# A decoder layer on one core: normed latents stored in full, and split where they are loaded

## The chip, the cores and the metric

The kernel runs on one core of a Trainium2 chip. A core has TensorE for matrix products (PE in the profile, its weight loads PEld), VectorE (DVE), ScalarE (ACT), GpSimd (POOL), and SyncE (SP), which here only issues DMAs; each works through its own queue of instructions in order and waits for the others by semaphores. The metric is the device time of one execution in microseconds (us); before the change it was 1661.43 us in the median of three runs.

## The reference

One layer of a decoder trunk on 1024 tokens of width 1024, all in float32: a norm with a conditioned scale and shift, two mixers side by side, a gated merge, a feed-forward part, a final norm. The part at hand is the second mixer, a latent attention:

```python
proj = h @ w_in
a_qkv, c_q, c_kv, k_r, gate_a, gate_b = jnp.split(proj, IN_SPLIT_POINTS, axis=-1)
y_a = _dilated_attention(a_qkv, rel_bias) @ w_up_a
y_b = _mla(c_q, c_kv, k_r, positions, g_q_lora, w_uq, g_kv_lora, w_ukv) @ w_up_b
...
# _mla
q = jnp.einsum('bsl,lhd->bshd', _rmsnorm(c_q, g_q_lora), w_uq)
kv = jnp.einsum('bsl,lhd->bshd', _rmsnorm(c_kv, g_kv_lora), w_ukv)
q_nope, q_rope = q[..., :M_NOPE], _rope(q[..., M_NOPE:], positions)
k_nope, v = kv[..., :M_NOPE], kv[..., M_NOPE:]
k_rope = _rope(k_r, positions)
```

The query latent `c_q` has 768 columns, the key/value latent `c_kv` 256: six and two pieces of 128. Both mixers have eight heads of width 64.

## The kernel before

A float32 operand is split into a high part, rounded to the format of the fast matrix product, and a low part, the rest; a product is three matmuls (high by high, high by low, low by high). `split` does this with a cast on ACT (line 83) and a subtraction on DVE, or on POOL where it is told so (line 84). A tile of 128 by 1024 float32 is 512 KB, half a tile (`hf`, 512 tokens) 256 KB.

Stage 1 is the input projection, in nine groups of two column pairs. Each pair is a Strassen product of seven (line 171: order 0, 1, 5, 4, 6, 3, 2), each with 12 matmuls at line 220. Products 5, 6 and 3 of a pair add up in one PSUM bank, and between them ACT or DVE copies out what has been reached (`plus`, `keep`). The right-hand operands lie in numbered cells of SBUF: product 4 reads cells 0 to 3, product 6 cells 4 to 7, product 3 cells 8 to 11, product 2 cells 12 to 15, product 5 cells 16 to 19. Sigmoid gates go to DRAM (`god`, line 399), and so do the latents. `cq_out` multiplies a piece of the query latent by its gain, splits it, and stores both parts in `nqd[0]` to `nqd[5]`. `kv_norm` does it for the two pieces of the key/value latent (`nqd[6]`, `nqd[7]`), normed in full.

Stage 2 is the attention: 16 heads (0 to 7 dilated, 8 to 15 latent), four units of 256 queries each, so units 0 to 63. A unit computes scores (`S`), exponentials on ACT (`P`), transposes (`tr`) and the product with the values (`pv`). A generator of fill work, `fill_a`, is drawn on during units 0 to 31 and puts other matmuls between (`acc`): `f_uk1` makes the keys of the latent heads in eight half tiles, `f_vb` their values in eight blocks of 128 tokens, stored to `vbd`, and `f_uq` their queries. Its operands are the latents, which `load_n` fetches into cells by way of POOL's DMA queue (`ldr`). `others` issues the loads of the next head at the second unit of each head, and at unit 1 the six query pieces and `k_rope`, which rotates the shared key. The key weight `wuk` is loaded by SP and split by ACT and POOL (`wk`).

The order of each engine's queue is not written by hand. A scheduler sorts the instructions by a timing model of its own and gives them their places; `tc.issue_after(x)` adds an edge from `x` to those instructions of the block that are on `x`'s engine.

Of the kernel before, what the change touches and what calls it, by code (L numbers as in the profile page):

```python
# [19 lines left out]
F32 = mybir.dt.float32  # L20
# [3 lines left out]
OP = mybir.AluOpType  # L24
# [20 lines left out]
def layer_kernel(ctx: ExitStack, tc: tile.TileContext, xT, c, pos, relT, wada, bada, gains, gq, gkv,  # L45
# [36 lines left out]
    def split(src, hi, lo, eng=DVE):  # L82
        ACT.copy(hi, src)  # L83
        eng.tensor_sub(lo, src, f32(hi))  # L84
# [52 lines left out]
    cqd = [dp.tile([P, T], F32, name=f"cqd{j}") for j in range(2)]  # L137
    nqd = [dp.tile([2, P, T], F32, name=f"nqd{j}") for j in range(8)]
    god = [dp.tile([P, T], F32, name=f"god{g}") for g in range(16)]
# [201 lines left out]
    def cq_out(src, j, hf, inplace):  # L341
        if hf not in acc:
            acc[hf] = SG()
            ACT.activation(acc[hf], src, AF.Square)
        else:
            t = X()
            ACT.activation(t, src, AF.Square)
            DVE.tensor_add(acc[hf], acc[hf], t)
        hi = X(F32R)
        lo = src.bitcast(F32R) if inplace else X(F32R)  # L350
        ACT.activation(hi, src, AF.Copy, scale=gql[:, j:j + 1])
        DVE.scalar_tensor_tensor(lo, src, gql[:, j:j + 1], f32(hi), op0=OP.mult, op1=OP.subtract)
        st(nqd[j][0][:, hsl[hf]], f32(hi))
        st(nqd[j][1][:, hsl[hf]], f32(lo))

# [291 lines left out]
    def kv_norm(hf, ts):  # L647
        a, b = SG(), f32(CHI())
        ACT.activation(a, ts[0], AF.Square)
        ACT.activation(b, ts[1], AF.Square)  # L650
        DVE.tensor_add(a, a, b)
        ps = trb()
        rms_rows(rms_cols([a], 256, ps), ps)
        for i, t in enumerate(ts):
            hi = CHI()
            DVE.scalar_tensor_tensor(t, t, gql[:, 6 + i:7 + i], ps, op0=OP.mult, op1=OP.mult)
            split(t, hi, t.bitcast(F32R))
            st(nqd[6 + i][0][:, hsl[hf]], f32(hi))
            st(nqd[6 + i][1][:, hsl[hf]], t)

# [59 lines left out]
    with ExitStack() as s2:  # L720
# [146 lines left out]
        wcols = lambda w: [t.rearrange("p (k f) -> p k f", f=P) for t in w]  # L867
        NHOME = (0, 2, 4, 6, 8, 10, 16, 18)
        nt = {}

        def load_n(j):
            t = [cell(NHOME[j] + l, [P, T]) for l in range(2)]
            for l in range(2):
                ldr(t[l], nqd[j][l])
            nt[j] = t

# [34 lines left out]

        OHOME = (12, 14, 16, 18)
        oa = {}
# [37 lines left out]
        def fill_a():  # L951
            small = [f_uk1(j, hf) for j in range(4) for hf in range(2)] + [f_vb(tb) for tb in range(8)]
            big = [f_uq(j, hf) for j in (4, 0, 1, 5, 2, 3) for hf in range(2)]
            pat = cycle("ssq")
            while small or big:
                kind = next(pat)
                src = small if kind == "s" and small or not big else big
                yield from src.pop(0)

# [7 lines left out]
        for j in (6, 7):  # L967
            load_n(j)
        cur["uk"] = wcols(wsplit(wuk, T, wraw(wuk, T, cell(4, [P, T], F32))))
        osum = {}  # L970
# [3 lines left out]
        def open_unit(u):  # L974
# [6 lines left out]
            units[u] = Unit(heads[idx], I, osum[0], 64 * (idx % 2), idx)  # L981

        def others(u):
            idx, I = u // 4, u % 4
            if I == 1 and idx < 15:
                heads[idx + 1] = load_head(*seq[idx + 1], (idx + 1) % 2)
            if u == 1:
                with tc.issue_after(v_ins[0].ins):
                    for j in (0, 1, 3, 4, 5, 2):
                        load_n(j)  # L990
                k_rope()

# [450 lines left out]
```

## Time and profile before

| | us |
|---|---|
| three runs | 1661.43, 1657.0, 1661.94 |
| the profiled execution | 1654.69 |
| its span | 1652.9 |
| PE busy | 1530.0 (93%) |
| DVE busy | 1237.9 (75%) |
| ACT busy | 828.9 (50%) |
| POOL busy | 549.9 (33%) |

Times inside the span count from its start. A row of the timeline gives the start, the duration, the engine, the line, the operation, output and inputs, and in brackets how long the engine stood idle before and what ended that. A row of the windows gives the length of a stretch and the busy time of each engine with its count of instructions, then the clock granted to PE (1.00 is full), the share of the DMA engines that was busy, and GB/s. A row of waits gives who waited for whom, the total in us, how many times, and the longest. Stage 1 ends near 434.5 us, and the dilated heads run from there to 657.6 us.

### The profile page before, as it was taken

Reading aid. Unit: us, or ns where it says so; the run is one execution under the profiler, and the core shown is the slowest. Engines: PE = TensorE matmul, PEld = TensorE weight load, DVE = VectorE, ACT = ScalarE, POOL = GpSimd, SP = SyncE. Lnnn points to the kernel's source line nnn. Section 1 sums busy time; section 2 is a strip of 40 time slices with the busy share of each in tenths; the row PEclk is TensorE's granted clock in tenths of the full one; section 3 lists DMA queues with packets and bytes.
Section 4 is the critical chain, followed back from the end, with each engine's and each line's share of the span. In section 5 each row is a group of like instructions: output and inputs, shape, how many; then the busy total and the mean of one; then the engine's idle time right before and its main releaser. Section 6 shows DMA issues by size and latency. Waiting matters only on the chain.

```text
span 1652.9 us, 22277 instructions
## 1 busy us (share of the span) xinstructions
PE 1530.0 (93%) x7306; PEld 1273.5 (77%) x7306; DVE 1237.9 (75%) x2443; ACT 828.9 (50%) x1631; POOL 549.9 (33%) x505
## 2 busy tenths in 40 slices
PE   4988999999769998999999997999999999899996
PEld 2757778878657887999978886778888888688885
DVE  7987997576267767889867669687767677688887
ACT  5842425444366867777734454434444444222325
POOL 0142333224243546434132015432332333233323
PEclk8989999999889999999999998999999999999998
DMA  9539675458996977766285342444444447966412
GB/s 336 187 120 328 241 254 198 146 185 240 284 228 171 220 200 203 181 164 153 69 307 202 133 141 73 169 185 179 159 148 160 166 145 283 393 251 256 176 41 102
DMA packets 175364, 321.40 MB, mean 194 GB/s; under 512 B 36988, under 2 KB 72492, under 8 KB 170000
## 3 DMA queue, kind: packets, MB, share of 16 engines
q1 hardware_dynamic: 107088, 241.22, 42.7%
q0 software_dynamic: 48000, 42.04, 12.0%
q10 hardware_dynamic: 20160, 36.71, 5.9%
q8 instruction: 58, 0.95, 0.2%
q14 instruction: 58, 0.48, 0.1%
HBM read 222.20 MB, written 102.34 MB: 196 GB/s over the span
## 4 chain that ended last, share of the span: by engine, by line
PE 49%; DVE 6%; DMA 6%; ACT 2%; issue 2%; POOL 1%; ACTq 0%; DVEq 0%; POOLq 0%; SPq 0%
PE bk L220 29%; PE acc L892 3%; PE S L783 3%; PE bk L87 3%; PE bk L89 3%; PE bk L88 3%; PE pv L824 2%; PE tr L805 2%; DMA vbd<-ev 2%; DMA tod<-x 1%; DMA cell<-tod 1%; DVE Wop L84 1%; DVE cell L84 1%; DMA Wraw<-wgate 1%; DVE x L278 1%
## 5 line engine op out<-in xcount | busy, mean ns | idle before, releaser
L220 PE MATMUL bk<-cell,Wop 128*128 128x512 f32 x4056 | 946.3, 395 | 44.7 <-DVE x L233 13.0
L220 PEld LDWEIGHTS bk<-cell,Wop 128*128 128x128 f32 x4056 | 769.3, 190 | 215.8 <-DVE Wop L84 11.5
L190 POOL TENSOR_TENSOR Wsum<-Wraw 128x512 f32<-128x512 f32 (+1 forms) x120 | 158.6, 1324 | 597.0 <-DVE Wop L84 377.3
L83 ACT CAST Wop<-Wsum 128x512 fp32r<-128x512 f32 (+1 forms) x241 | 130.0, 548 | 220.1 <-PE bk L220 159.4
L83 ACT CAST Wop<-Wraw 128x512 fp32r<-128x512 f32 (+2 forms) x182 | 107.6, 593 | 173.5 <-PE bk L220 99.5
L84 DVE TENSOR_TENSOR Wop<-Wsum,Wop 128x512 fp32r<-128x512 f32 (+1 forms) x241 | 157.8, 663 | 46.7 <-ACT Wop L83 46.1
L84 DVE TENSOR_TENSOR Wop<-Wraw,Wop 128x512 fp32r<-128x512 f32 (+2 forms) x182 | 138.6, 765 | 34.5 <-ACT Wop L83 32.2
L783 PE MATMUL S<-cell,cell 128*128 128x128 f32 (+8 forms) x480 | 120.0, 365 | 13.1 <-DMA cell<-ksd 8.3
L1245 DVE SCALAR_TENSOR_TENSOR x<-bk,modc,x 128x512 f32<-128x512 f32 x140 | 103.5, 747 | 35.8 <-PE bk L220 30.9
L790 ACT ACTIVATE P<-P,mx 128x512 f32<-128x512 f32 (+7 forms) x128 | 99.4, 779 | 34.9 <-DVE mx L785 21.6
L84 DVE TENSOR_TENSOR pl<-tr,ph 128x512 fp32r<-128x512 f32 (+1 forms) x160 | 98.4, 630 | 24.3 <-ACT ph L83 23.4
L892 PE MATMUL acc<-cell,w 128*128 128x512 f32 x408 | 112.7, 404 | 0.1
L190 POOL TENSOR_TENSOR Wsum<-Wraw,Wsum 128x512 f32<-128x512 f32 (+1 forms) x60 | 79.7, 1335 | 68.4 <-DVE Wop L84 66.2
L805 PE MATMUL tr<-ident,P 128*128 128x128 f32 x576 | 94.6, 282 | 6.0 <-ACT P L793 5.3
L783 PEld LDWEIGHTS S<-cell,cell 96*128 96x128 f32 (+1 forms) x480 | 80.8, 197 | 22.1 <-DMA cell<-ksd 8.8
L824 PE MATMUL pv<-ph,v 128*128 128x256 f32 (+1 forms) x320 | 88.5, 293 | 5.1 <-ACT ph L83 4.3
L87 PE MATMUL bk<-cell,Wop 128*128 128x512 f32 (+1 forms) x240 | 91.3, 380 | 1.9 <-ACT Wop L83 1.9
L83 ACT CAST ph<-tr 128x512 fp32r<-128x512 f32 (+1 forms) x160 | 83.3, 544 | 17.2 <-PE tr L805 14.5
L88 PE MATMUL bk<-cell,Wop 128*128 128x512 f32 (+1 forms) x240 | 90.5, 378 | 0.0
L89 PE MATMUL bk<-cell,Wop 128*128 128x512 f32 (+1 forms) x240 | 89.9, 378 | 0.0
L163 ACT COPY x<-bk 128x512 f32<-128x512 f32 x92 | 52.4, 585 | 68.8 <-PE bk L220 46.9
L892 PEld LDWEIGHTS acc<-cell,w 128*128 128x128 f32 x408 | 76.5, 193 | 13.4 <-DVE ev L923 0.4
(254 smaller groups left out, 2217.8 us busy)
## 6 DMA issues: line engine op xcount, KB each, us to landing
tod<-x ACTq DMA_DIRECT2D x140, 256.0 KB, 2.7
cell<-tod SPq DMA_DIRECT2D x70, 512.0 KB, 6.9
Wraw<-win SPq DMA_DIRECT2D x18, 1024.0 KB, 6.7
Wraw<-wgate SPq DMA_DIRECT2D x11, 1024.0 KB
Wraw<-wup SPq DMA_DIRECT2D x11, 1024.0 KB, 6.0
Wraw<-wdown SPq DMA_DIRECT2D x20, 512.0 KB, 5.2
ada<-wada SPq DMA_DIRECT2D x16, 512.0 KB, 6.3
cm<-wada SPq DMA_DIRECT2D x32, 256.0 KB, 3.3
```

Of the source, the lines that this page charges most:

```text
L83: ACT.copy(hi, src)
L84: eng.tensor_sub(lo, src, f32(hi))
L87: PE.matmul(ps, w[0], a[0], start=first, stop=False)
L88: PE.matmul(ps, w[0], a[1], start=False, stop=False)
L89: PE.matmul(ps, w[1], a[0], start=False, stop=last)
L190: POOL.tensor_tensor(t, a, b, op=op)
L220: PE.matmul(ps, w[:, wi, k], t[k][:, ti], start=start and k == 0 and n == 0, stop=k == self.nk - 1 and n == 2, skip_group_check=True)
L783: anchor[0] = PE.matmul(s, q[:, i * P:i * P + P], k[:, c * wd:c * wd + wd], start=pi == 0, stop=pi == len(passes) - 1)
L805: anchor[0] = PE.transpose(tr[:, co:co + P], self.p[a][:, kb * P:kb * P + P], ident)
L824: anchor[0] = PE.matmul(pv[:, o if l else 0:], v[:, kk], p[:, l:r], start=kk == 0 and n == 0, stop=last and l > 0 and n == 1, skip_group_c ...
L892: PE.matmul(ps, w[wi][:, k0 + k], act(k, ai, hf), start=k == 0 and n == 0, stop=k == nk - 1 and n == 2)
L1245: DVE.scalar_tensor_tensor(xs, self.bk[name], modc[:, 40 + j:41 + j], xs, op0=OP.mult, op1=OP.add)
```

## The change

`cq_out` and `kv_norm` no longer split: they store the scaled piece once, in full. `load_n` fetches one tile in place of two, into the second cell of its pair, and `split_n` splits it there, the high part into the first cell. Pieces 6 and 7 are loaded and split at the start. The six others are loaded at units 1, 2, 3, 4, 6 and 7, and split three units later. The pieces have other cells (`NHOME`), the key weight is loaded into cell 12, `k_rope` stands at unit 12, and `fill_a` yields the whole key and value work before the queries, where it took two small pieces and one big one in turn.

```diff
-    nqd = [dp.tile([2, P, T], F32, name=f"nqd{j}") for j in range(8)]
+    nqd = [dp.tile([P, T], F32, name=f"nqd{j}") for j in range(8)]
...
-        hi = X(F32R)
-        lo = src.bitcast(F32R) if inplace else X(F32R)
-        ACT.activation(hi, src, AF.Copy, scale=gql[:, j:j + 1])
-        DVE.scalar_tensor_tensor(lo, src, gql[:, j:j + 1], f32(hi), op0=OP.mult, op1=OP.subtract)
-        st(nqd[j][0][:, hsl[hf]], f32(hi))
-        st(nqd[j][1][:, hsl[hf]], f32(lo))
+        t = src if inplace else X()
+        ACT.activation(t, src, AF.Copy, scale=gql[:, j:j + 1])
+        st(nqd[j][:, hsl[hf]], t)
...
-        a, b = SG(), f32(CHI())
+        a, b = SG(), CM()
...
-            hi = CHI()
             DVE.scalar_tensor_tensor(t, t, gql[:, 6 + i:7 + i], ps, op0=OP.mult, op1=OP.mult)
-            split(t, hi, t.bitcast(F32R))
-            st(nqd[6 + i][0][:, hsl[hf]], f32(hi))
-            st(nqd[6 + i][1][:, hsl[hf]], t)
+            st(nqd[6 + i][:, hsl[hf]], t)
...
-        NHOME = (0, 2, 4, 6, 8, 10, 16, 18)
+        NHOME = (0, 2, 6, 16, 18, 4, 8, 10)
...
         def load_n(j):
-            t = [cell(NHOME[j] + l, [P, T]) for l in range(2)]
-            for l in range(2):
-                ldr(t[l], nqd[j][l])
-            nt[j] = t
+            nt[j] = t = [cell(NHOME[j] + l, [P, T]) for l in range(2)]
+            ldr(f32(t[1]), nqd[j])
+
+        def split_n(j):
+            split(f32(nt[j][1]), *nt[j])
...
-        OHOME = (12, 14, 16, 18)
+        OHOME = (12, 14, 8, 10)
...
-            pat = cycle("ssq")
-            while small or big:
-                kind = next(pat)
-                src = small if kind == "s" and small or not big else big
-                yield from src.pop(0)
+            for g in small + big:
+                yield from g
...
         for j in (6, 7):
             load_n(j)
-        cur["uk"] = wcols(wsplit(wuk, T, wraw(wuk, T, cell(4, [P, T], F32))))
+            split_n(j)
+        cur["uk"] = wcols(wsplit(wuk, T, wraw(wuk, T, cell(12, [P, T], F32))))
...
+        NU = {1: 0, 2: 1, 3: 3, 4: 4, 6: 5, 7: 2}
+
...
-            if u == 1:
-                with tc.issue_after(v_ins[0].ins):
-                    for j in (0, 1, 3, 4, 5, 2):
-                        load_n(j)
-                k_rope()
+            with tc.issue_after(anchor[0].ins):
+                if u in NU:
+                    load_n(NU[u])
+                if u - 3 in NU:
+                    split_n(NU[u - 3])
+                if u == 12:
+                    k_rope()
```

Two queues show where the scheduler put this. First POOL at the end of stage 1, before the change: `nqd6` and `nqd7` are the key/value pieces, `nqd0` to `nqd5` the query pieces, `ksd0` a key of the dilated heads, and `wk1` the low part of the key weight.

```order
L874 DMA cell16_3968<-nqd6_104 128x1024
L874 DMA cell17_3969<-nqd6_104 128x1024
L874 DMA cell18_3972<-nqd7_105 128x1024
L874 DMA cell19_3973<-nqd7_105 128x1024
L874 DMA cell0_4034<-nqd0_98 128x1024
L874 DMA cell1_4035<-nqd0_98 128x1024
...
L874 DMA cell9_4047<-nqd4_102 128x1024
L84 TENSOR_TENSOR wk1_3979<-cell4_3976,wk0_3978 128x1024
```

The same place after the change:

```order
L740 DMA cell26_3976<-ksd0_75 128x1x1024
L190 TENSOR_TENSOR Wsum_3846<-Wraw_3575,Wsum_3692 128x512
L867 DMA cell17_4079<-nqd3_101 128x1024
L867 DMA cell19_4137<-nqd4_102 128x1024
L867 DMA cell1_3985<-nqd0_98 128x1024
L867 DMA cell3_4027<-nqd1_99 128x1024
L867 DMA cell5_4351<-nqd5_103 128x1024
L867 DMA cell7_4419<-nqd2_100 128x1024
L867 DMA cell9_3917<-nqd6_104 128x1024
L867 DMA cell11_3922<-nqd7_105 128x1024
L84 TENSOR_TENSOR wk1_3929<-cell12_3926,wk0_3928 128x1024
```

All eight loads have moved together to this place, and the two key/value pieces from the head of the row to its end.

Second ACT at the same place, before the change. `Wop` is a weight's high part for a Strassen product, `x<-bk` copies a PSUM bank out, `x<-x` is a sigmoid, and `P0` the first exponential.

```order
L83 CAST Wop_3879<-Wsum_3877 128x512
L83 CAST Wop_3900<-Wsum_3898 128x512
L163 COPY x_3812<-bk_3632 128x512
L398 ACTIVATE x_3814<-x_3814 128x512
L163 COPY x_3835<-bk_3650 128x512
...
L83 CAST wk0_3978<-cell4_3976 128x1024
L398 ACTIVATE x_3874<-bk_3650 128x512
...
L790 ACT_TABLE_LOAD
```

And after it, where the casts from one cell to its neighbour are `split_n`:

```order
L83 CAST Wop_3827<-Wsum_3825 128x512
L83 CAST cell16_4078<-cell17_4079 128x1024
L83 CAST Wop_3848<-Wsum_3846 128x512
L83 CAST cell18_4136<-cell19_4137 128x1024
L83 CAST cell0_3984<-cell1_3985 128x1024
L163 COPY x_3760<-bk_3580 128x512
L83 CAST cell2_4026<-cell3_4027 128x1024
...
L163 COPY x_3783<-bk_3598 128x512
...
L83 CAST cell10_3921<-cell11_3922 128x1024
L784 ACT_TABLE_LOAD
...
L83 CAST wk0_3928<-cell12_3926 128x1024
```

The eight casts stand ahead of the table load for the first exponential, three of them ahead of the copy of bank `bk_3580` and four ahead of that of `bk_3598`, and the cast of the key weight has moved behind the table load.

On PE the matmuls of the fill work move between the heads: counted in PE's order from the first score of one head to that of the next, heads 0 to 7 hold 6, 24, 36, 36, 54, 52, 44 and 42 of them before, and 12, 30, 30, 42, 54, 47, 37 and 42 after; in both, 18 more stand behind head 8's first score.

## The prediction

> **What bounds the kernel now.** I read the windows first, cut at the first score matmul of each attention head; the phase of eight dilated heads (0 to 7) runs from 434.5 to 657.6 us.
>
> ```profile
> core 0: us, PE busy (x) PEld busy (x) DVE busy (x) ACT busy (x) POOL busy (x), PEclk, DMA share, GB/s
> 434.50:457.90 23.40, 12.24 (x57) 9.93 (x55) 9.60 (x39) 11.40 (x25) 7.79 (x12) 0.71 1.16 320
> 457.90:486.40 28.50, 23.41 (x116) 19.17 (x116) 24.45 (x68) 20.97 (x43) 17.50 (x16) 0.88 1.05 239
> 486.40:524.30 37.90, 26.80 (x154) 23.72 (x152) 20.97 (x58) 20.49 (x46) 11.77 (x12) 0.86 0.62 164
> 524.30:546.80 22.50, 21.82 (x137) 19.28 (x137) 19.80 (x59) 18.87 (x41) 8.35 (x9) 1.00 0.77 225
> 546.80:573.00 26.20, 25.58 (x158) 22.71 (x156) 18.83 (x58) 21.13 (x49) 15.53 (x18) 1.00 0.97 219
> 573.00:602.90 29.90, 27.14 (x152) 22.22 (x152) 16.85 (x56) 21.31 (x50) 14.13 (x18) 1.00 0.75 196
> 602.90:633.80 30.90, 25.84 (x144) 22.77 (x144) 19.60 (x62) 22.34 (x50) 14.02 (x15) 0.89 0.78 190
> 633.80:657.60 23.80, 23.10 (x145) 20.20 (x143) 19.51 (x56) 16.64 (x39) 16.62 (x22) 1.00 0.81 208
> ```
>
> In head 0 TensorE (PE) works 12 of 23 us with the DMA engines full (share 1.16), and head 2 takes 37.9 us where head 3 takes 22.5. The waits of PE name the reasons, the first three between 434 and 560 us, the last between 600 and 665 us.
>
> ```profile
> PE acc L892 <- POOL wk L84: 8.0, 1, 8.0
> PE S L783 <- DMA cell<-ksd: 7.7, 1, 7.7
> PE acc L892 <- DMA cell<-nqd: 2.9, 2, 2.4
> PE tr L805 <- ACT P L793: 5.0, 1, 5.0
> ```
>
> The 8.0 us is the split of the key weight on GpSimd (POOL), which stands behind 13 of the 16 latent loads in POOL's queue. The 7.7 us is head 2's key, behind the last of them. The 5.0 us ends at ScalarE (ACT); the chain of waits puts it to a value store ahead of it:
>
> ```profile
> 577.18 14.27 DMA vbd<-ev
> 610.20 12.67 DMA vbd<-ev
> ```
>
> So the phase suffers from late loads first, and from late value stores later. When loads land is read from POOL's timeline: it uses eight semaphores in turn, so each load waits until the one eight places ahead has landed.
>
> ```profile
> 411.15 1.22 POOL L874 DMA_DIRECT2D cell<-nqd  x2 [0.47 <-PE bk L220]
> 423.73 0.53 POOL L874 DMA_DIRECT2D cell<-nqd  x1 [11.36 <-DMA cell<-ksd]
> 436.43 0.53 POOL L874 DMA_DIRECT2D cell<-nqd  x1 [1.28 <-DMA cell<-ksd]
> 437.64 0.53 POOL L874 DMA_DIRECT2D cell<-nqd  x1 [0.68 <-DMA cell<-nqd]
> 444.38 0.53 POOL L874 DMA_DIRECT2D cell<-nqd  x1 [1.45 <-DMA cell<-nqd]
> 444.93 2.35 POOL L84 TENSOR_TENSOR wk<-cell,wk 128x1024 fp32r<-128x1024 f32 x1
> ```
>
> Head 0's query had landed by 423.7, head 1's last key by 436.4, and the first latent tile, issued at 411.15, shortly after 437: 26 us in the queue. From 437.64 to 444.38 four more land, 1.7 us apart.
>
> **The change, part by part.** Stores of the first stage: 12 scale-and-subtract instructions on VectorE (DVE), 4 casts and 4 subtractions of the key/value pieces and 16 stores go.
>
> ```profile
> 246.00:320.00 74.00, 74.00 (x333) 61.24 (x333) 52.23 (x83) 37.34 (x74) 23.05 (x16) 1.00 0.49 169
> ```
>
> Where the twelve stand PE is busy 74.00 of 74.00 us, so they are covered by PE and their removal brings 0 (bounds -2 and +2 us for the rest of the stage, which is written in another order).
>
> Loads: 16 of 512 KB become 8, that is 4.2 MB less before head 2's load.
>
> Splits: 8 casts on ACT and 8 subtractions on DVE of 128x1024 come in. By intent they come three units after their loads. But the block that places them ties instructions of PE's queue only, and they run on others: the order shows all eight ahead of the first exponential, four of them in front of copies that the last input pair needs. An ACT cast that waits holds up what is behind it, as this shows:
>
> ```profile
> 421.08 0.59 ACT L163 COPY x<-bk 128x512 f32<-128x512 f32 x1 [2.04 <-PE bk L220]
> 423.81 0.59 ACT L163 COPY x<-bk 128x512 f32<-128x512 f32 x1 [0.74 <-PE bk L220]
> 433.85 1.05 ACT L83 CAST wk<-cell 128x1024 fp32r<-128x1024 f32 x1 [6.73 <-DMA cell<-wuk]
> 434.80 0.59 ACT L398 ACTIVATE x<-bk 128x512 f32<-128x512 f32 x1
> 436.45 1.28 ACT L790 ACT_TABLE_LOAD   x1
> ```
>
> The two copies at 421.08 and 423.81 free the banks of products 6 of the last pair; product 3 accumulates into the same bank and waits for the copy. In the changed order the first copy stands behind the splits of tiles 3, 4 and 0, the second behind that of tile 1. So PE, which now passes 423.8 without a pause, will stop there.
>
> How long: tile 3 is the ninth load on POOL, as the first latent tile is now. Until it lands, two sorts of transfer fall away, since they wait for the stopped engines or for a later cell:
>
> ```profile
> 421.76 0.33 SPq L855 DMA_DIRECT2D cell<-wuk  x1
> 423.09 13.72 SPq L399 DMA_DIRECT2D god<-x  x6
> 430.00:435.00 5.00, 4.82 (x23) 3.90 (x21) 1.01 (x2) 1.15 (x2) 0.66 (x2) 1.00 1.09 347
> 440.00:445.00 5.00, 0.00 (x0) 0.00 (x0) 0.00 (x0) 0.66 (x2) 1.66 (x4) 0.50 1.11 402
> 450.00:455.00 5.00, 5.00 (x26) 4.57 (x26) 3.67 (x15) 3.54 (x9) 0.53 (x1) 0.67 1.28 269
> ```
>
> That is 0.5 and six times 0.25 MB. At the 347 GB/s of 430 to 435 the 2.0 MB take 5.8 us; part would have come after the tile, so I take 4.5 and a landing at 432.8. Bounds: 431 (all of it gone) and 437.3 (none). Tiles 4 and 0 follow at 1.7 us each, 436.2; one cast (1.05) and the copy (0.59) end at 437.8. PE stops 14.0 us (bounds 12.2 and 18.5).
>
> A rule of the Trainium skill bears on this choice ("DMA: Bandwidth & Descriptors", "Queues, rings and completion order"): each DMA engine takes turns between the queues that have work. By it an empty SP queue leaves the engines to POOL's loads, and the landing is the early one; if POOL's queue kept its present pace, the landing would be 437.3 and the sum 4.5 us worse. No run here shows that yet.
>
> Then four products remain. PE's rate is in this row:
>
> ```profile
> 403.66 30.99 PE L220 MATMUL bk<-cell,Wop 128*128 128x512 f32 x136
> 437.27 0.47 PE L892 MATMUL acc<-cell,wk 128*128 128x512 f32 x1 [2.45 <-DMA cell<-nqd]
> 447.33 0.79 PE L892 MATMUL acc<-cell,wk 128*128 128x512 f32 x1 [8.02 <-POOL wk L84]
> ```
>
> 30.99/136 is 0.228 us, and 48 matmuls take 10.9 us. After the idle stretch the granted clock is 0.50 and still 0.67 at 450 to 455, after idling for most of 435 to 447; I add 2.5 us (five us at half speed; bounds 1 and 4). The stage ends at 451.2 in place of 434.7.
>
> The key/value tiles come last on POOL, not first: their cells (8 to 11) are free only when the last product 3 has read them, near 447.2 and 448.6. Three rows price what follows.
>
> ```profile
> cell<-tod SPq DMA_DIRECT2D x70, 512.0 KB, 6.9
> 437.74 0.40 ACT L790 ACTIVATE P<-P,mx 128x128 f32<-128x128 f32 x1
> L84 DVE TENSOR_TENSOR Wop<-Wsum,Wop 128x512 fp32r<-128x512 f32 (+1 forms) x241 | 157.8, 663 | 46.7 <-ACT Wop L83 46.1
> ```
>
> A 512 KB load takes 6.9 us to land at the median; the DMA engines are emptier here, so I take 5 (bounds 2 and 7): the second tile is in at 453.5, its cast done at 454.5, the table load (1.28) at 455.8, the first exponential (0.40 and a read of its sum, some 0.6) and the key weight's cast (1.05) at 457.5. The first filler matmul, which stands behind that cast, runs then, ten us behind the 447.3 at which it now gets going. **Loss at the entry: 10 us** (bounds 7 and 15). The DVE subtractions, some 1.3 us each by twice the 663 ns of a 128x512 one, lie in that wait.
>
> Heads: with the latents in and half of the bytes gone, I rebuild each head from the nearest head of the windows; the filler matmuls per head, counted in the order, are 6, 24, 36, 36, 54, 52, 44, 42 before and 12, 30, 30, 42, 54, 47, 37, 42 after. Head 0's rest costs 3 more (6 fillers, 1.4 us, and exponentials that pile up behind the splits). Head 1: 24 in place of 28.5, since the key rotation leaves its DVE, busy 24.45 of 28.5 us. Head 2: 27 for 37.9, the 7.7 gone and a full clock. Head 3: 28 for 22.5, since it takes half of the value blocks and the rotation. Head 4 26.5, head 5 25 (29.9 with value blocks), head 6 24.5 (30.9, the 5.0 gone), head 7 23.8. Heads 1 to 7 sum to 178.8 against 199.7: **20.9 us less** (bounds 8 less, only the 7.7 us, and 35 less, all at 23.5). The key rotation, now after head 2, is needed by head 8 alone, which hides it; were it late, head 8's load would wait.
>
> Sum: 10 + 3 - 20.9 = -7.9, and 0.5 for the first stage: -8.4 us. The profiled execution took 1654.69 us (span 1652.9 and 1.8 around it), so 1646.3. It lies 6.7 below the median of the runs, 1661.43; taken to that median, 1653.0 us.
>
> **The rivals.** *Nothing left (25 in 100).* The heads don't fall to 25 us. Without the named waits heads 1 to 7 average (199.7-7.7-5.0)/7 = 26.7 us, 187 in all, 12.7 less, which the entry's 13 us eats: 1661. For it: heads 4 and 5 run at 26 to 30 us with hardly a wait. Against: heads 3 and 7 run at 22.5 and 23.8 with as many fillers.
>
> *Slower (17).* The value blocks, now spread over heads 4 to 6, fall into heads 2 and 3, four blocks and eight 256 KB stores a head. The stores just quoted (14.27 and 12.67 us) held ACT and cost PE 5.0 us at once; with twice as many in a head each block may wait for its buffer. Four such stops beyond those now are 20 us, 1673. It decides from two on, 10 us. Against: both stores came while a head's loads were under way.
>
> *Much faster (12).* The loads land early enough that the entry costs 5 us or less, or the heads run at PE's own pace of 22.5 us: 15 to 25 less, 1641 on average. Against: 26 us in the queue.
>
> *The likeliest (46):* the entry loses what is computed, the heads gain more: 1653, its own range 1644 to 1658.
>
> Faster by over 0.3% (5 us, about what a measurement here tells from no change): 46 + 12, 0.58; within, 0.25; slower, 0.17. The range 1638 to 1668 reaches into the last two rivals and leaves out their ends.
>
> **What would show it.** Right: PE idle 12 to 18 us from near 424, ACT waiting there in a 128x1024 cast for a load from nqd; the first filler matmul near 457; no wait for ksd at head 2; head 8 starting near 649 in place of 657.6. Wrong: no pause of PE at 424 (the loads came early), or ACT waiting for vbd stores in heads 2 and 3 for over 10 us, or heads that stay near 27 us.

## The result: 1674.7 us, slower by 0.9%, and the profile after

| | before | after |
|---|---|---|
| median of four runs, us | 1659.22 | 1674.67 |
| lowest and highest, us | 1656.54, 1661.94 | 1672.0, 1678.09 |
| ratio, 95% interval | 1 | 1.0091 [1.0072, 1.0110] |
| the profiled execution, us | 1654.69 | 1678.09 |
| start of head 0, from the trace | 434.5 | 456.7 |
| start of head 8 | 657.6 | 679.7 |
| from there to the end of the span | 995.3 | 996.6 |

The forecast was 1653.0 us (1638 to 1668) and faster; the time lies above the range. The profiled execution of before lies below its median and that of after is the slowest of its four, so the traces stand 23.4 us apart where the medians stand 15.5 apart. In the traces the difference is simple: 22.2 us to the start of head 0, -0.1 us in heads 0 to 7, 1.3 us behind them. In the experiments below one execution, of held_kv, took 8562.84 us where its three others took 1670.54 to 1674.6, and is left out of its ratio.

The windows of the changed kernel: first the pause of PE at the end of stage 1 and its restart in two steps, then heads 0 to 7, then these eight in one row.

```profile
core 0: us, PE busy (x) PEld busy (x) DVE busy (x) ACT busy (x) POOL busy (x), PEclk, DMA share, GB/s
427.86:442.93 15.07, 0.00 (x1) 0.00 (x1) 3.01 (x4) 4.09 (x6) 2.11 (x4) 0.63 0.96 232
442.93:446.35 3.42, 3.42 (x8) 2.75 (x9) 3.38 (x4) 2.00 (x3) 0.00 (x0) 0.50 0.15 55
446.35:449.77 3.42, 3.42 (x11) 2.69 (x11) 1.36 (x2) 2.88 (x4) 0.00 (x0) 0.63 0.35 131
456.70:477.70 21.00, 12.46 (x56) 10.16 (x55) 12.79 (x39) 13.54 (x26) 4.03 (x2) 0.76 0.48 154
477.70:501.30 23.60, 22.31 (x146) 19.69 (x145) 22.37 (x67) 20.62 (x45) 8.03 (x10) 1.00 0.86 242
501.30:525.50 24.20, 20.68 (x133) 18.22 (x132) 19.79 (x55) 21.48 (x50) 10.45 (x12) 1.00 0.91 239
525.50:559.40 33.90, 26.33 (x145) 22.20 (x144) 19.04 (x57) 21.82 (x52) 13.02 (x17) 0.90 0.74 197
559.40:604.80 45.40, 31.31 (x155) 26.76 (x154) 26.52 (x67) 21.86 (x47) 24.63 (x23) 0.77 0.52 143
604.80:628.70 23.90, 23.84 (x150) 21.27 (x148) 19.77 (x55) 18.15 (x40) 13.19 (x13) 1.00 0.88 182
628.70:655.30 26.60, 23.42 (x133) 19.73 (x130) 19.77 (x57) 18.97 (x43) 12.23 (x11) 0.94 0.81 189
655.30:679.70 24.40, 23.86 (x153) 21.14 (x152) 19.12 (x58) 19.21 (x43) 17.65 (x24) 1.00 0.78 197
456.70:679.70 223.00, 184.22 (x1053) 159.16 (x1051) 159.18 (x451) 155.66 (x339) 103.22 (x107) 0.91 0.73 189
```

Against the same table of before, head 2 fell from 37.9 to 24.2 us, as the prediction said, but head 3 rose from 22.5 to 33.9 (28 forecast) and head 4 from 26.2 to 45.4 (26.5 forecast), its clock at 0.77. The waits of PE that lead the list between 425 and 680 us:

```profile
PE bk L220 <- ACT x L163: 15.1, 1, 15.1
PE pv L818 <- ACT ph L83: 12.1, 2, 10.3
PE S L777 <- DVE mx L779: 8.2, 6, 3.1
PE acc L887 <- ACT wk L83: 6.5, 1, 6.5
PE acc L87 <- ACT ev L934: 5.7, 3, 4.9
PE S L777 <- DMA cell<-ksd: 2.2, 1, 2.2
```

Four of the six are PE waiting for ACT, among them the three longest single waits. Selected rows of the timelines say what ACT waits for, first at the entry (the two PE rows are the end of the pause and the first filler matmul, POOL's row is the load of the second key/value piece):

```profile
438.84 1.04 ACT L83 CAST cell<-cell 128x1024 fp32r<-128x1024 f32 x1 [18.43 <-DMA cell<-nqd]
442.30 0.58 ACT L163 COPY x<-bk 128x512 f32<-128x512 f32 x1
442.93 13.92 PE L220 MATMUL bk<-cell,Wop 128*128 128x512 f32 x48 [15.07 <-ACT x L163]
454.43 0.53 POOL L867 DMA_DIRECT2D cell<-nqd  x1 [0.83 <-PE bk L220]
456.74 1.05 ACT L83 CAST cell<-cell 128x1024 fp32r<-128x1024 f32 x1 [1.45 <-DMA cell<-nqd]
463.09 1.04 ACT L83 CAST cell<-cell 128x1024 fp32r<-128x1024 f32 x1 [4.78 <-DMA cell<-nqd]
465.85 1.03 ACT L83 CAST wk<-cell 128x1024 fp32r<-128x1024 f32 x1
466.93 1.22 PE L887 MATMUL acc<-cell,wk 128*128 128x512 f32 x2 [6.54 <-ACT wk L83]
```

Then in head 4. The query rope works on two halves of the tokens, and each half takes two multiplications (L840, L841) and a sum (L842) on POOL. The rows are both multiplications of the first half, the first one of the second half, the sum of the first half, ACT's cast of that sum, and PE:

```profile
578.23 1.29 POOL L840 TENSOR_TENSOR ev<-ev 128x512 f32<-128x512 f32 x1 [6.22 <-DMA ev<-cst]
585.45 1.26 POOL L841 TENSOR_TENSOR ev<-ev 128x512 f32<-128x512 f32 x1 [4.14 <-DMA ev<-cst]
589.82 1.26 POOL L840 TENSOR_TENSOR ev<-ev 128x512 f32<-128x512 f32 x1 [3.10 <-DMA ev<-cst]
591.03 1.26 POOL L842 TENSOR_TENSOR ev<-ev 128x512 f32<-128x512 f32 x1
592.33 0.62 ACT L83 CAST ev<-ev 128x512 fp32r<-128x512 f32 x1 [12.74 <-POOL ev L842]
593.38 0.58 PE L818 MATMUL pv<-ph,v 128*128 128x256 f32 x1 [10.33 <-ACT ph L83]
```

The chain of waits has, in the same places, a start and a duration for each transfer:

```profile
454.43 8.64 DMA cell<-nqd
530.44 14.93 DMA vbd<-ev
571.88 13.58 DMA krd<-ev
585.48 4.18 DMA ev<-cst
```

The two ropes share the seven `EV` buffers. The rotary key's store (`krd`) ends at 571.88 + 13.58 = 585.46, and a table of the query rope's second half (`cst`) is loaded from 585.48: it had to wait for that buffer. The multiplication that needs it stands in POOL's queue ahead of the first half's sum, and ACT, in order, holds the cast of that sum ahead of the `ph` copy that PE needs. Not all of ACT's 12.74 us are this buffer's. The first half's second table came in only at 585.45; it had been issued at 571.23, as soon as the rotary keys' last sum on POOL was done (569.92 + 1.28). From there the two instructions of the first half need 2.5 us, so without the second half ahead of it the sum could have ended near 588.0 in place of 592.3; this is an estimate from these rows.

### The profile page after: what moved, and what is told of

It is laid out like the page before. It is cut to its first block, busy times and chain, and to the rows that moved or that the text cites. A ratio compares the mean times of both kernels' runs of the same rounds, so it can differ in the third digit from the quotient of the medians.

```text
span 1676.3 us, 22179 instructions
## 1 busy us (share of the span) xinstructions
PE 1536.4 (92%) x7306; PEld 1279.2 (76%) x7306; DVE 1242.8 (74%) x2435; ACT 834.6 (50%) x1635; POOL 546.5 (33%) x497
## 3 DMA queue, kind: packets, MB, share of 16 engines
q0 software_dynamic: 46848, 37.84, 10.8%
## 4 chain that ended last, share of the span: by engine, by line
PE 60%; DMA 15%; DVE 13%; issue 4%; ACT 4%; POOL 2%; SPq 1%; ACTq 0%; DVEq 0%; POOLq 0%
PE bk L220 38%; PE acc L887 4%; PE S L777 3%; DMA cell<-ksd 3%; PE bk L87 3%; PE bk L88 3%; PE bk L89 3%; PE pv L818 3%; PE tr L799 2%; DVE Wop L84 2%; DMA vbd<-ev 1%; DVE cell L84 1%; DMA cl<-wada 1%; DMA tod<-x 1%; DMA cell<-tod 1%
## 5 line engine op out<-in xcount | busy, mean ns | idle before, releaser
L818 PE MATMUL pv<-ph,v 128*128 128x256 f32 (+1 forms) x320 | 88.9, 294 | 12.2 <-ACT ph L83 12.1
L163 ACT COPY x<-bk 128x512 f32<-128x512 f32 x92 | 52.5, 584 | 68.3 <-PE bk L220 46.2
```

What stands on the lines that cost most here:

```text
L818: anchor[0] = PE.matmul(pv[:, o if l else 0:], v[:, kk], p[:, l:r], start=kk == 0 and n == 0, stop=last and l > 0 and n == 1, skip_group_c ...
```

## The experiments

Each theory explains the same 15 us. *Queue theory*: ACT stands in order behind early splits, and the entry costs it all. *Place theory* (first called rope theory): the rotary keys at unit 12 cost it, by meeting the query rope or by their place alone. *Fill theory*: the filler's order does. The rivals (landing, give-back) say that a wait only moves. *Collision theory* is the place theory's rival that late rotary keys cost only beside a query rope. All kernels compute the reference in full. Ratios are to the kernel before, run beside each; the difference of two kernels' ratios is uncertain by some 0.002 to 0.003. The last three columns are from the traces, in us, one execution each. The stretch behind head 8, which the edits hardly touch, takes 990.8 to 997.8 us in these traces, so a few us between two traces need not be the edit's.

| kernel | ratio, 95% interval | head 0 starts | heads 0 to 7 | PE busy in them |
|---|---|---|---|---|
| before | 1 | 434.5 | 223.1 | 185.9 |
| after | 1.0091 [1.0072, 1.0110] | 456.7 | 223.0 | 184.2 |
| rope_early | 1.0069 [1.0039, 1.0098] | 451.7 | 216.1 | 185.1 |
| split_held | 1.0110 [1.0083, 1.0137] | 435.9 | 232.4 | 185.7 |
| held_kv | 1.0103 [1.0077, 1.0129] | 457.5 | 222.7 | 183.9 |
| rope_late_only | 1.0073 [1.0050, 1.0096] | 435.2 | 236.2 | 190.1 |
| entry_free | 1.0033 [1.0017, 1.0048] | 445.3 | 225.7 | 187.4 |
| entry_rope | 1.0041 [1.0024, 1.0057] | 443.2 | 222.1 | 189.1 |
| entry_rope_mix | 0.9966 [0.9951, 0.9981] | 441.6 | 212.7 | 185.4 |
| entry_rope_ssq | 1.0076 [1.0056, 1.0096] | 446.3 | 226.2 | 187.8 |
| mix_only | 1.0101 [1.0083, 1.0119] | 453.7 | 223.5 | 187.6 |
| before_seq | 1.0012 [0.9999, 1.0025] | 437.3 | 223.7 | 185.3 |
| before_mix | 0.9978 [0.9959, 0.9997] | 434.2 | 222.8 | 185.1 |
| gate_mix | 1.0003 [0.9988, 1.0018] | 439.2 | 223.4 | 190.2 |
| before_seq_rope | 1.0046 [1.0025, 1.0066] | 435.7 | 230.4 | 187.7 |
| kv_split_seq | 1.0021 [1.0002, 1.0040] | 436.9 | 224.4 | 190.1 |
| kv_split_mix | 0.9923 [0.9899, 0.9947] | 440.0 | 215.5 | 186.6 |
| rope6_mix | 0.9941 [0.9916, 0.9966] | 445.3 | 211.9 | 186.0 |
| rope6_kv_split_mix | 0.9931 [0.9906, 0.9957] | 437.4 | 215.7 | 183.5 |

### Taking the change back, one suspect at a time

**rope_early.**

```diff
-                if u == 12:
+                if u == 1:
                     k_rope()
```

> The changed kernel with the rotary keys back at unit 1, all else as it is. Rope theory: the 18 to 19 us that head 4 takes above its neighbours (45.4 us against 24 to 27) come from the rotary keys' work meeting the query rope there for the EV buffers, so head 4 falls to about 27 us, heads 0 and 1 pay 2 to 5 us for it, and the time is 1657 to 1662 us (13 to 17 us below the changed kernel's 1674.7). Fill theory (rival): heads 3 and 4 are long because the eight value blocks and the big pieces now follow each other, wherever the rotary keys stand; then head 4 keeps over 35 us and the time stays above 1669 us.

Head 4 kept 46.2 us, so its length alone proves nothing: it now holds 84 filler matmuls (54 after) and PE works 36.0 us in it. The wait behind the rope did shrink, and the eight heads took 216.1 in place of 223.0:

```profile
573.34 0.62 ACT L83 CAST ev<-ev 128x512 fp32r<-128x512 f32 x1 [5.35 <-POOL ev L842]
```

The ratio fell by 0.0022, within its uncertainty. The place theory as I had written it failed; so did the reading of a head's duration as its cost. The time, 1666.3 us, met neither range: the fill theory had it above 1669.

**split_held.** The scheduler ties an instruction only to one on the same engine, so the six query splits are tied to ACT's latest exponential (`expa`).

```diff
+                expa[0] = ACT.activation(t[:, :n], t[:, :n], AF.Exp, ...)
...
                 if u - 3 in NU:
-                    split_n(NU[u - 3])
+                    with tc.issue_after(expa[0].ins):
+                        split_n(NU[u - 3])
```

> The changed kernel with each of the six query latents' splits held behind the latest exponential on ScalarE, so that none stands ahead of the last bank copies of stage 1; loads and cells are unchanged. Queue theory: the 15.07 us pause of TensorE for the bank copy goes to below 3 us, head 0's first filler matmul comes 12 to 16 us earlier than 466.9, and the time is 1659 to 1664 us. Landing theory (rival): the entry is set by the key and value pieces and the head's keys landing late, so the pause moves behind stage 1 and at most 5 us come back: 1669 us or more.

The pause went and stage 1 ended where it did before. The time didn't move. ACT and PE at the start of head 0:

```profile
445.61 1.04 ACT L83 CAST cell<-cell 128x1024 fp32r<-128x1024 f32 x1 [10.79 <-DMA cell<-nqd]
448.17 1.86 PE L777 MATMUL S<-cell,cell 128*128 128x384 f32 x4 [11.63 <-DVE mx L779]
```

The first exponentials now stand behind ACT's wait for the key/value pieces: 11.63 of 15.07 us moved over the border into head 0. The landing theory foretold that the time stays. (In the traces head 8 starts 11.4 us earlier than after, but that execution is the fastest of its four.)

**held_kv.** The same, and the key/value pieces in the cells that come free first.

```diff
-        NHOME = (0, 2, 6, 16, 18, 4, 8, 10)
+        NHOME = (0, 2, 4, 6, 8, 10, 16, 18)
-        OHOME = (12, 14, 8, 10)
+        OHOME = (12, 14, 16, 18)
-        cur["uk"] = wcols(wsplit(wuk, T, wraw(wuk, T, cell(12, [P, T], F32))))
+        cur["uk"] = wcols(wsplit(wuk, T, wraw(wuk, T, cell(4, [P, T], F32))))
```

> As the kernel with the held splits, and the key and value pieces in the cells that come free first (16 to 19), the raw key weights in cell 4, so that these pieces are loaded first; the key and value splits still stand ahead of the last two bank copies. Queue theory: ScalarE waits for these two pieces in the place where it waited for the query pieces, a pause of 8 to 14 us at the end of stage 1, but head 0's filler starts right behind: 1 to 5 us above or below the kernel with the held splits, 1656 to 1666 us. Landing theory: what counts is how early the two pieces are on the chip, so it gains 8 us or more on the kernel with the held splits alone.

```profile
444.44 13.24 PE L220 MATMUL bk<-cell,Wop 128*128 128x512 f32 x48 [14.11 <-ACT x L163]
```

The pause came back, now for these two pieces, and head 0 was short (13.0 us). The time stayed, above what the queue theory allowed, and the 8 us or more that the landing theory promised over split_held didn't come either (1.0103 and 1.0110): each theory failed here.

**entry_free.** Now the key/value splits too are tied, to the last bank copy (`kept`).

```diff
+        kept[0] = ACT.copy(t, ps)
...
             load_n(j)
-            split_n(j)
+            with tc.issue_after(kept[0].ins):
+                split_n(j)
```

> The changed kernel with the whole entry freed: the query splits held behind the latest exponential, the key and value pieces in the cells that come free first (16 to 19), and their two splits held behind the last bank copies of stage 1. The rotary keys stay at unit 12. Queue theory: stage 1 ends at about 435 us of the profile as in the kernel before (456.7 in the changed one), head 0's first filler matmul comes within 5 us of it, heads 0 to 7 take about the 223 us that they took in the changed kernel, and the time stands at 0.997 to 1.002 of before. Give-back theory (rival): the heads are bound by something that the entry only moves (their DMA loads and the pieces' buffers), so heads 0 to 7 take 230 us or more and the time stays at 1.006 or above, as it did with the held splits alone.

0.0058 came back, 9.6 us of 1658, and the time lies between the two expectations. The three edits together brought it, where the first alone and the first two brought nothing; the last without the cells wasn't run. Head 0 still starts 10.8 us later than before, 5.49 of it here, since ACT's casts that wait for the pieces (11.46 us) also stand ahead of the last gate activations:

```profile
445.27 0.69 PE L779 MATMUL S<-cell,cell 128*128 128x128 f32 x2 [5.49 <-ACT x L397]
```

**entry_rope** is entry_free with `k_rope` at unit 1.

> As the kernel with the freed entry, and the rotary keys back at unit 1. Place theory: late rotary keys cost 4 to 12 us by themselves (they did in the kernel before with that part alone), so heads 0 to 7 take 212 to 217 us and the time is 5 to 9 us below the freed entry: 0.992 to 0.997 of before. Rival: the rotary keys at unit 1 meet the key and value pieces and the first heads' loads, and heads 0 to 2 give back what heads 3 to 7 gain: within 3 us of the freed entry.

No gain, and the rival's reason: heads 3 and 4 fell by 11.6 us, but head 1, where three of the query splits stand too, rose from 25.8 to 34.0, its clock from 0.93 to 0.80:

```profile
457.30:491.30 34.00, 23.41 (x129) 20.45 (x128) 24.36 (x67) 24.47 (x49) 15.34 (x14) 0.80 0.69 187
```

### One part of the change on the kernel before

**rope_late_only.**

```diff
+            if u == 12:
                 k_rope()
```

> The kernel before with one part of the change alone: the rotary keys at unit 12 instead of unit 1. Its filler mixes small and big pieces, so the query rope of piece 4 is long done by then and that of piece 5 comes later. Collision theory: late rotary keys cost only where a query rope stands beside them; here the time is within 5 us of before (1655 to 1664 us). Place theory (rival): rotary keys in the middle of the heads cost by themselves, some 10 to 19 us, since their stores hold buffers that the filler needs: 1669 to 1678 us.

12 us, within the place theory's 10 to 19 (the time, 1667.2 us, ends below its 1669, beside a kernel before that ran at 1655.5) and well beyond the collision theory's 5. But the trace doesn't bear out the reason. ACT's and PE's longest waits, and the first load of the rotary keys:

```profile
518.02 0.62 ACT L83 CAST ev<-ev 128x512 fp32r<-128x512 f32 x1 [12.75 <-POOL ev L848]
519.89 1.11 PE L783 MATMUL S<-cell,cell 128*128 128x448 f32 x2 [10.62 <-DVE mx L785]
534.43 0.52 SPq L882 DMA_DIRECT2D ev<-krr  x1
```

The wait is behind the query rope in head 2, and the rotary keys are not even loaded then, so they can't hold its buffers. Heads 1 and 2 took 8.4 us more than before and heads 3 to 7 7.8 more. What makes moved rotary keys cost 12 us in this order stays open.

**before_seq** has the changed order alone (`for g in small + big: yield from g`).

> The kernel before with one part of the change alone: all key pieces and value blocks first, then the query pieces. Fill theory: the eight value blocks in a row wait for the buffers that their stores hold, 4 to 10 us above before (1.003 to 1.006). Rival: this order is what the change gains by, as the first query piece's wait for weights (8.0 us) goes from head 0: 3 to 8 us below before (0.995 to 0.998).

Nothing that can be told from 0; neither expectation was met. **before_seq_rope** adds `if u == 12` ahead of `k_rope()` to it.

> The kernel before with two parts of the change: key pieces and value blocks first, and the rotary keys at unit 12; latents stored split, as before. With the order alone the time stood at 1.0012 of before. Place theory: late rotary keys make ScalarE wait 11 to 13 us for a rotary tile or its store in head 3 or 4 (12.74 us in the changed kernel, 10.90 us with the freed entry, 11.10 us with the alternating order) and that costs 5 to 12 us here: 1.004 to 1.009 of before. Rival: in this order the wait is there and PE has other work, so that it costs nothing, as the freed entry with early and late rotary keys took the same time: 0.999 to 1.003.

0.0034 more, 5.6 us, as the place theory had it; the wait of PE that leads the list between 430 and 665 us, and ACT's timeline:

```profile
PE pv L824 <- ACT ph L83: 16.9, 4, 10.8
```

```profile
578.72 0.62 ACT L83 CAST ev<-ev 128x512 fp32r<-128x512 f32 x1 [13.15 <-POOL ev L848]
```

The chain of waits has the same pair as in the changed kernel, the query rope's table loaded when the rotary keys' store has landed:

```profile
557.29 14.59 DMA krd<-ev
571.90 4.14 DMA ev<-cst
```

So 10.8 us of idle PE in head 4 arise with every latent stored split, and before_seq has no such wait. It belongs to the rotary keys in the new order and not to the storing.

### The order of the filler

**entry_rope_mix** is entry_rope with this, **entry_rope_ssq** the same with the old order (`ssq`) in place of the last lines:

```diff
+        NU = {1: (0, 1, 3, 4, 5, 2)}
+        SU = {1: (0, 1), 2: (3, 4), 3: (5, 2)}
...
+            keys = [f_uk1(j, hf) for j in range(4) for hf in range(2)]
+            vals = [f_vb(tb) for tb in range(8)]
...
-            for g in small + big:
+            for g in keys + [g for p in zip(vals, big) for g in p] + big[8:]:
                 yield from g
```

> As the kernel with the freed entry and early rotary keys, with another filler order: the key pieces first, then value blocks and query pieces by turns, all six query loads at unit 1 and their splits at units 1 to 3. Fill theory: eight value blocks in a row wait for the buffers that their stores hold (some 8 us of PE waiting for ScalarE's copies of them), and by turns this wait falls below 3 us: 4 to 8 us below the kernel with the same entry. Rival: the waits only move to the query pieces: within 3 us of it.

> As the kernel with the freed entry and early rotary keys, with the filler order of the kernel before (two small pieces, one big), the query loads at unit 1 and their splits at units 1 to 3. What is left of the change is then that the latents are stored whole and split where they are loaded. Fill theory: this order is as good as the alternating one, 0.990 to 0.996 of before. Rival: a query piece in head 0 or 1 waits for its weights and latents (8.0 us and 2.9 us in the profile of before), which the order with the key and value pieces first avoids: 3 to 8 us above the kernel with that order.

By turns, the time fell by 12 us below entry_rope, more than expected, to below the kernel before; heads 0 to 7 take 212.7 us with 27.3 idle (33.0). PE's waits for ACT's copies of the filler fell from 11.5 to 1.4 us, and those for the value blocks (L936), of which the fill theory spoke, from 4.8 to none. Since this run also moves the loads and splits of the query pieces, entry_rope_ssq is the fairer comparison: it differs in the order alone and is 0.0110 slower. With the old order the same storage costs 0.0076; the rival foretold the sign, not the size, and of its reasons only the weights show. PE waits 6.40 us in head 0 behind ACT, which waits 7.04 us for a query weight to land, and 8.07 us in head 2 behind the query rope; no wait of PE in these heads is put down to the split of a latent. The eight heads in the alternating order, then in the old one:

```profile
441.60:654.30 212.70, 185.40 (x1052) 161.32 (x1052) 152.23 (x455) 159.10 (x344) 105.91 (x110) 0.91 0.80 201
446.30:672.50 226.20, 187.79 (x1052) 161.69 (x1052) 159.37 (x454) 157.91 (x341) 103.30 (x108) 0.88 0.74 188
```

**mix_only** is the changed kernel with that order, loads at unit 1 and splits at units 1 to 3, unheld.

> The changed kernel with the filler order alone replaced: the key pieces first, then value blocks and query pieces by turns; for that the six query loads stand at unit 1 and their splits at units 1 to 3, unheld, so that they stand ahead of the last bank copies as in the changed kernel. Cells and rotary keys (unit 12) as changed. Fill theory: the order is worth the 12 us between the two kernels with the freed entry, so the time is 0.997 to 1.003 of before, with the pause of 11 to 16 us at the end of stage 1 still there. Rival: the order is worth something only with early rotary keys and a freed entry, since late rotary keys meet the value blocks and query pieces: 1.005 or above.

No gain, as the rival said. Its pause is 13.9 us, and ACT waits 11.10 us for a `krd` store in head 4. **before_mix** is the kernel before with the alternating order.

> The kernel before with the alternating filler order alone (keys first, then value blocks and query pieces by turns), the latents stored split as before. If the order alone makes the fast version, this one stands at 0.992 to 0.997 of before, and storing the latents whole is worth nothing. If the latents' halved traffic has a part in it, this one stays within 0.997 to 1.003.

The order alone has 3.6 us, in the range of the second expectation; the interval ends at 0.9997, so it can hardly be told from no change.

### Which latents cost, and what is left to gain

**gate_mix** is entry_rope_mix with the key/value splits and the key weight's tied to the last gate activation, not the last copy.

> As the fast kernel (freed entry, early rotary keys, alternating order), with the key and value splits and the key weights' split held behind the last gate activation of stage 1 instead of the last bank copy. In the trace of the fast kernel ScalarE waited 9.95 us for the first key and value piece with four gate activations behind it, and TensorE's first scores waited 4.0 us for these. Queue theory: that 4.0 us wait goes, the first scores start at 437 to 438 us instead of 441.55, and the time falls by 2 to 5 us (0.993 to 0.996 of before). Rival: the head's keys, not yet landed, take its place, and the time stays as it is (0.996 to 0.998).

The 4.0 us wait went, as expected, and yet 6 us were lost, which neither expectation had. An idle time of 8.02 us came into head 0, with ACT idle 8.46 us ahead of a query weight's cast; what releases that cast, the trace doesn't name.

```profile
462.43 0.83 ACT L83 CAST w<-wraw 128x768 fp32r<-128x768 f32 x1 [8.46 <-issue]
464.57 0.48 PE L801 MATMUL tr<-ident,P 128*128 128x128 f32 x1 [8.02 <-ACT P L789]
```

**kv_split_seq** and **kv_split_mix** store key/value latents split as before, in entry_rope and in entry_rope_mix.

```diff
+    nqd = [dp.tile([P, T] if j < 6 else [2, P, T], F32, name=f"nqd{j}") for j in range(8)]
...
+            if j < 6:
+                ldr(f32(t[1]), nqd[j])
+            else:
+                for l in range(2):
+                    ldr(t[l], nqd[j][l])
```

> As the kernel with the freed entry and early rotary keys (1.0041 of before), with the key and value latents stored split as in the kernel before, so that nothing is split at the entry; the query latents are stored whole and split behind the exponentials. Key-and-value theory: what was left of the cost of storing whole (4.8 us to the kernel before with the same order, 1.0012) is the entry's wait of ScalarE for these two pieces (12.09 us), so this stands at 1.000 to 1.002. Query theory (rival): what is left lies in heads 0 and 1, where six query splits are added on ScalarE and VectorE (head 1 took 34.0 us with 10.6 us idle), so it stays at 1.003 to 1.005.

> The same storage (key and value latents split, query latents whole) with early rotary keys and the alternating order. Key-and-value theory: 3 to 6 us below the kernel with all latents whole in that order (0.9966): 0.992 to 0.995 of before, the fastest here. Query theory: within 0.002 of it.

In the first the gain of 0.0020 is not beyond its uncertainty. In the second it is 0.0043, 7 us, and the kernel is the fastest by its median ratio: 1649.0 us where before took 1659.3, and 0.0055 below before_mix. Storing the six query latents whole does pay, once nothing at the entry waits for a split and the order gives the query pieces time. In the traces heads 0 to 7 take some 7 us less than in before_mix and start some 6 us later; the traced execution of before_mix is one of its fastest, so they show less than the medians.

**rope6_mix** is entry_rope_mix with the rotary keys at unit 6, **rope6_kv_split_mix** is kv_split_mix with that.

> The fast kernel (freed entry, alternating order, all latents whole) with the rotary keys at unit 6 instead of unit 1, between the query splits of head 0 and 1 and the query rope of head 3. If head 1's 34.9 us with 10.8 us idle come from the rotary keys meeting the query splits, head 1 falls to 25 to 28 us and the time by 3 to 8 us (0.992 to 0.995 of before). Rival: unit 6 meets the value blocks' stores and the wait only moves to heads 2 and 3: 0.996 or above.

> The two best parts together: key and value latents stored split, query latents whole, alternating order, and the rotary keys at unit 6. If the two gains (0.9966 to 0.9923 by the split key and value latents, 0.9966 to 0.9941 by unit 6) lie in different places, the entry and head 1, they add up: 0.988 to 0.991 of before. Rival: both are taken from the same idle time of heads 0 and 1, and the time stays within 0.002 of 0.9923.

rope6_mix met its expected time. In both, head 1 fell (34.9 to 28.0, and 32.8 to 26.6 us) and head 2 rose (20.0 and 20.4 to 26.9 and 26.5), with clocks of 0.81 and 0.87 there. Heads 1 and 2 of rope6_mix:

```profile
459.60:487.60 28.00, 24.56 (x146) 20.98 (x145) 26.21 (x73) 26.16 (x53) 7.26 (x9) 0.94 0.85 217
487.60:514.50 26.90, 17.57 (x100) 15.32 (x98) 17.36 (x54) 16.10 (x38) 11.03 (x10) 0.81 0.57 157
```

The gain of 0.0025 is at the edge of what can be told, and in the traces it isn't in the eight heads (212.0 us, 212.7 without it). The two gains don't add: there the rival was right.

## Why the prediction was wrong

**Where the 15 us are.** Two chains of runs lead from one kernel to the other. Forward: the order 2.0 us, the late rotary keys 5.6, whole latents with their cells and unheld splits 7.5 (ratios 1.0012, 1.0046, 1.0091, times 1658). Backward: the entry 9.6, early rotary keys -1.3, split key/value latents 3.3, split query latents 1.5, the order 2.0. Each part is uncertain by 2 to 5 us, so only 5.6, 7.5 and 9.6 stand clear of zero. The parts depend on each other: late rotary keys cost 5.6 us on the kernel before with the new order and 12 with its own, and nothing (-1.3) where the query splits stand in head 1, in which early ones are done.

**The pause: right.** PE stopped 15.07 us (14.0 forecast, 12.2 to 18.5), for the copy behind the casts, as described. The size is in part luck: the first cast ran 10.98 us after PE stopped (9.0 forecast, worked out at 347 GB/s where the DMA engines then moved 217), but the copy followed it by 3.46 us and not by 4.4. The two readings of the queues gave 9.0 and 13.5. A rule of the Trainium skill ("DMA: Bandwidth & Descriptors", "Queues, rings and completion order": engines take turns between queues that have work) spoke for the early one; the measurement lies between the two and doesn't decide on that rule.

**The restart: right.** The four products took 13.77 us where 13.4 were forecast; the clock was 0.50 and 0.63 for the first 6.8 us.

**The entry: mis-sized.** The first filler matmul ran at 466.93, not 457.5: 19.6 us late, not 10. Stage 1 stood 4.1 us behind already (427.86 in place of 423.8). I held the removed DVE work to be covered and allowed 2 us for the new order; the 0.5 us that the sum takes off for this stage has no row behind it, and no run shows it. How much of the 4.1 is the change's I can't say. 1.4 of it is there at 221 us, before the first latent is stored, and before_seq and before_seq_rope, which leave stage 1 alone, end it up to 2.8 us apart from before. PE's wait for DVE near 391 us (1.67) is no sign either: a like one at 369 us (1.99) is gone, and before_seq has one of 1.01 us at 391. The second key/value piece was issued at 454.43 (448.6 forecast) and took 8.64 us to land (5 forecast, bounds 2 and 7).

**The heads: the step that failed.** Heads 1 to 7 were to take 20.9 us less than before (bounds 8 and 35); they took 202.0 us (679.7 - 477.7), not 178.8, and so 2.3 more. That is 23.2 of the 31.8 us by which the traces miss the sum. Head 2's wait for `ksd` fell from 7.7 to 2.2 (to none, by the forecast) and heads 1 to 3 took 81.7 (79 forecast), near enough. (Head 5 of before starts at 572.16, not at the 573.0 of its row; that moves 0.8 us from head 4 to head 5.) Head 4 took 45.4, not 26.5, and no other head missed by over 6 us. I had moved the rotary keys out of head 1 as a gain of DVE time, and said that only head 8 waits for them. I didn't count what they hold on the way: `EV` buffers until slow stores land, and places in the queues of POOL and ACT. before_seq_rope shows that wait, and its 5.6 us, without the rest of the change. It isn't the whole miss: rope_early, where the rotary keys are done in heads 0 and 1, still has a long head 4 and gains only 0.0022. Over the eight heads the idle time of PE stayed as it was, 37.2 us before (223.1 - 185.9) and 38.8 after (223.0 - 184.2): the waits that I took out went, and others came in their place. How much each of the others costs by itself stays open.

**The rivals.** "Slower" had the sign and the time (1673) but not the mechanism: value stores held ACT for 5.79 us in head 3, and PE waited 5.7 us in all for their blocks, where it asked for 20. "Nothing left" was nearer on the heads (187 us for heads 1 to 7), but still had them gain 12.7 us and the entry lose 13, where the traces have 2.3 us more in those heads and 19.8 ahead of them. Of the signs of being wrong one came: the heads stayed near 27 us (202.0 / 7 is 28.9). The error behind both is one: I rebuilt each head from its nearest neighbour, and a wait that goes doesn't leave the sum if another instruction in the same queue waits next.

## What to carry to other kernels

An instruction that waits for a transfer holds its whole in-order queue, so a cast moved to the place of a load has to be tied on the engine that runs it, behind what the bottleneck needs next; here two such ties and other cells were in place before any of the time came back. How far behind has to be tried: gate_mix, where the key weight's split too was tied one step further back, lost 6 us. When work is moved, count what it holds while it waits (buffers, queue places), and not its busy time alone. Judge a phase by its sum: single heads moved by 14 to 19 us here, down and up, with the eight together at 223 us as before.

## What the runs showed that I had not expected

Idle time of PE was paid a second time in clock here: the granted clock was 0.63 over the pause, 0.50 in the 3.4 us after it, and 0.77 over head 4 with its 14 us of idle time. Unlike kernels spent 212 to 236 us in heads 0 to 7, while PE's busy time in them stayed within 183 to 191. And halving what the latents move (8.4 MB less of 324 read and written) bought nothing at the entry: no kernel here with its key/value latents whole starts head 0 earlier than before.
